# Recurrent layer of a two-layer encoder: the 19 dense-weight loads issued by ScalarE instead of SyncE

## The chip, the core and the metric

The kernel runs on one core of one Trainium2 chip, in one launch. The metric is device time in microseconds (us), the median of the runs shown; lower is better. The core has five engines that work at the same time, each taking its own instructions in the order of its own queue: TensorE (in the profile PE, with its weight loads as PEld), VectorE (DVE), ScalarE (ACT), GpSimd (POOL) and SyncE (SP). SyncE computes nothing here; it begins transfers. GpSimd begins those transfers that add to what they write. An engine that begins a transfer spends a short instruction on it, called the issue here; the data lands later, and whoever reads it waits for the landing.

## The reference, cut to what matters

The input is x (512 tokens of 1024 values). Layer 0 mixes tokens with a recurrence over 12 heads of 64, in parallel with an attention of 4 heads into 256 memory tokens; layer 1 does the same with chunked attention in place of the recurrence. Each layer ends in an output projection and a gated feed-forward block.

```python
h = rms_norm(x, ln1[0])
p = h @ a_w_in[0]                      # r, k, v of the recurrence, and the memory queries
def step(state, inp):                  # for each of the 512 tokens, 12 heads
    r_t, w_t, k_t, v_t, a_t, b_t = inp
    sa = einsum('bhvk,bhk->bhv', state, a_t)
    state = (state * w_t[:, :, None, :] + sa[..., None] * b_t[:, :, None, :]
             + v_t[..., None] * k_t[:, :, None, :])
    return state, einsum('bhvk,bhk->bhv', state, r_t)
mix = group_norm(y) * ... * g
mo  = memory_attention(q_mem, mem_n, w_mem_kv[0])
x = x + concatenate([mix, mo]) @ w_out[0]
x = x + conv_glu(rms_norm(x, ln2[0]), ...)
```

The change touches only layer 0 up to its output projection: the part with `a_w_in`, and the first two column tiles of `w_out[0]`.

## The kernel before, in words

**Dense products.** A weight tile is 128 x 1024 values of float32 (512 KB). It is loaded into a buffer called `wraw` (two buffers, so a load may begin when the reader of the tile before last has finished). `split_w` (lines 204 to 221) then makes two tiles from it: `whi`, a copy rounded to TensorE's float32 format, by ScalarE (line 207), and `wlo`, the rest. There are two ways to the rest. With `lo` off, VectorE subtracts (`wlo` = raw - `whi`, line 215). With `lo` on, ScalarE writes the raw tile, scaled by -1 and rounded (line 212) and GpSimd begins a transfer that adds the same weight tile from memory to it (line 213), so VectorE has no part in it. `whi` and `wlo` have three buffers each. `dense` (line 248) then issues 16 matmuls with `whi` (lines 257 and 258) and 8 with `wlo` (line 261) into one bank of results (`psd`).

**Where a load is begun.** `raw_w` (line 224) allocates the `wraw` buffer and issues the load, always on SyncE (line 226). `load_w` calls it and splits.

**The recurrent layer.** The 12 heads are six pairs. Per pair there are three generators: `prepare` (three projections k, r and v, each with its own weight tile; decay, keys, bonus), `front` and `back` (the chunked form of the recurrence, in many small matmuls). `weave` traces a step of whichever generator is furthest behind its share of the estimated cost. In stage st (0 to 4) it weaves `front` of pair st, `prepare` of pair st+1 and `back` of pair st-1. A last weave holds the two last `back`s, the last `front`, two projections for the memory queries (`q_mem`), the memory attention and two of the eight tiles of the output projection (`out_ahead`). In `prepare`, a projection takes the tile that was loaded ahead and asks for the next one (line 1174 and following) before its own matmuls are traced.

**Who orders the queues.** The traced order is only a preference: the framework draws up the queue of each engine from dependencies, free buffers and priorities. `tc.issue_after`, `tc.keep_in_program_order` and `tc.high_priority` are the kernel's own marks for places where that order is held down.

**The switch `lo_on`.** `lo_on[0]` is 0 at first, set to 1 at line 1596 before stage 0 and back to 0 at line 1635 after the last weave. While it is 1, `load_w` takes the second way to `wlo` (`prepare` passes `lo` itself: for the first two tiles of the second pair it is off).

**The small transfers.** `keys` turns a small triangular system through DRAM: ScalarE copies blocks into `Lc` (line 1235), eight small transfers write them to `d` (line 1238), four read them back re-arranged as `Lr` (line 1244), VectorE runs a recursion of 15 steps on `Lr` and `X` (lines 1246 to 1266, tiles `Xu`, `Xsa`, `Xsb`), four transfers write `X` to `d2` (line 1272) and four read it back as `Tc` (line 1276), which `front` uses. Also `wa` (line 1154), `g2` (line 1470) and the mixer's result (`mixd`, line 1527) go through SyncE's queue, as did the weight loads.

Of the kernel before, what the change touches and what calls it, by code (L numbers as in the profile page):

```python
# [133 lines left out]
def trunk_kernel(ctx, tc, A, out):  # L134
    nc = tc.nc
    PE, V, SC, GP = nc.tensor, nc.vector, nc.scalar, nc.gpsimd
# [5 lines left out]
    def wtile(name, dt=F32R, tag=None, at=None, slot=None):  # L142
        if name in turns:
            n = turns[name] if slot is None else slot
            while (name, n) in held:
                n = (n + 1) % 3
            turns[name] = (n + 1) % 3
            tag = f"{name}{n}"
            at = W_AT[name] if at is None else at
        else:  # L150
            at = at or 0
        t = wp.tile([P, 1056], dt, name=name, tag=tag or name, bufs=1 if name in turns else 2)
        return t[:, at:at + 1024]
# [47 lines left out]
    lo_on = [0]  # L201
    raw_at = [None]
# [20 lines left out]

    def raw_w(src, n=1024):
        raw = wtile("wraw", F32)
        raw_at[0] = nc.sync.dma_start(raw[:, :n], src)
        return raw[:, :n]

    def load_w(src, n=1024, lo=None, at=None):
        return split_w(raw_w(src, n), n, src if (lo_on[0] if lo is None else lo) else None, at=at)  # L230
# [204 lines left out]
    def ffn(l, hp, U, T, new_x, xT, after=None, tokens=None):  # L435
# [199 lines left out]
        def ending():  # L635
            j = NFF - 1
            last7 = made[j - 1]
            src = A["ffn_in"][l, j]
            made[j - 2].end2()
            wg = split_w(raw_w(src[0]), 1024, None, keep, hold=True)  # L640
            yield
            wg[2]()
# [9 lines left out]
            pg = ps_d()  # L652
            run(dense(pg[:], [(wg[:2], KO)], pair_of(Uh, Ul)))
            wv_raw = raw_w(src[1])
            last7.end1()
            last7.endr()
# [922 lines left out]
    with tc.issue_after(norm_at[0].ins):  # L1579
# [5 lines left out]
        for m in range(KD):  # L1585
            src = memT[m // 4][:, m % 4]
# [470 lines left out]
```

## Time and profile before

| | us |
|---|---|
| median of 3 runs (lowest, highest) | 1273.2 (1271.75, 1273.56) |
| the profiled execution | 1271.7 |
| its span (first to last instruction) | 1269.9 |
| VectorE busy in the span | 1031.8 |
| ScalarE busy in the span | 839.7 |
| GpSimd busy in the span | 151.2 |

The profile is of one execution, so sums are made against its 1271.7 us and then moved to the median. A busy time does not count issues of transfers, branches or semaphores. In a list of waits, a line says which engine and line sat idle, which instruction ended that, the total in us, how often, and the longest. In a timeline, a row is: start, duration, engine, line, operation, tiles, count; a bracket at the end holds the idle time before it and what ended it. A row with a count above 1 merges neighbours. "DMA to landing" is the time from the issue until the data is there.

### The profile page before, as it was taken

To read this page: it belongs to the slowest core of one execution; us is meant where nothing else is said; L and a number is where in the kernel's file an instruction comes from. 1 tells how busy PE (TensorE), PEld (TensorE's weight loads), DVE (VectorE), ACT (ScalarE), POOL (GpSimd) and SP (SyncE) were. 2 spreads that over 40 slices of the span, in tenths; PEclk is the share of its full clock that TensorE was granted. 3 is DMA by queue.
4 is the path that set the end of the run, shared out by engine and by line. 5 is a ranking of instruction groups with operands and counts; after the bars stand their busy time and mean duration, and the time that the engine had idled before them with its cause. 6 is when DMAs were issued, how large, how long until landed. Compare 5 with 4: busy or idle time off the path is not lost.

```text
span 1269.9 us, 26429 instructions
## 1 busy us (share of the span) xinstructions
PE 1227.0 (97%) x10420; PEld 1077.7 (85%) x10420; DVE 1031.8 (81%) x1958; ACT 839.7 (66%) x1396; POOL 151.2 (12%) x180
## 2 busy tenths in 40 slices
PE   9999999999998999999999999999999999999997
PEld 7787777777788999999888878777789999998886
DVE  7976677765678999999886976658889999999785
ACT  6567668756466777776664676767767777765662
POOL 1000000000001222220120000000002322211200
PEclk9999999999999999999999999999999999999999
DMA  6355444353064889885994332233428899977971
GB/s 207 102 171 119 96 107 92 83 118 102 6 194 114 195 214 204 201 204 131 304 223 130 108 101 67 84 108 133 133 50 192 212 208 196 201 165 254 245 178 67
DMA packets 95293, 191.10 MB, mean 150 GB/s; under 512 B 22080, under 2 KB 30400, under 8 KB 95168
## 3 DMA queue, kind: packets, MB, share of 16 engines
q1 hardware_dynamic: 68592, 129.14, 31.9%
q0 software_dynamic: 26576, 60.26, 27.0%
q8 instruction: 82, 1.34, 0.4%
q14 instruction: 43, 0.35, 0.1%
HBM read 173.15 MB, written 6.29 MB: 141 GB/s over the span
## 4 chain that ended last, share of the span: by engine, by line
PE 46%; DVE 23%; ACT 11%; issue 10%; DMA 10%; SPq 0%; POOL 0%; ACTq 0%; DVEq 0%; POOLq 0%
PE psf L718 7%; DMA wlv<-in_ffn_in_dram 5%; PE psd L261 4%; PE psf L723 3%; PE psf L452 3%; PE psd L257 3%; PE psd L258 3%; PE psd L718 3%; ACT whi L517 2%; DVE wlo L215 2%; PE psf L454 2%; DVE raw L504 2%; DVE wlo L522 2%; PE psd L723 1%; DVE raw L513 1%
## 5 line engine op out<-in xcount | busy, mean ns | idle before, releaser
L517 ACT CAST whi<-raw 128x1024 fp32r<-128x1024 f32 (+1 forms) x168 | 151.0, 939 | 52.1 <-DVE raw L509 26.4
L452 PE MATMUL psf<-th,whi 128*128 128x256 f32 x672 | 159.6, 276 | 4.2 <-ACT tmp L573 2.1
L452 PE MATMUL psf<-tl,whi 128*128 128x256 f32 x672 | 159.1, 275 | 0.0
L452 PEld LDWEIGHTS psf<-th,whi 128*128 128x128 f32 x672 | 128.8, 192 | 5.3 <-ACT tmp L573 2.8
L207 ACT CAST whi<-wraw 128x1024 fp32r<-128x1024 f32 x84 | 87.3, 1045 | 66.8 <-PE psd L258 33.9
L452 PEld LDWEIGHTS psf<-tl,whi 128*128 128x128 f32 x672 | 129.0, 192 | 0.0
L522 DVE TENSOR_TENSOR wlo<-raw,whi 128x1024 fp32r<-128x1024 f32 (+1 forms) x108 | 109.0, 1011 | 6.5 <-ACT whi L517 6.5
L257 PE MATMUL psd<-r1h,whi 128*128 128x512 f32 x264 | 104.1, 395 | 0.1
L258 PE MATMUL psd<-r1l,whi 128*128 128x512 f32 x264 | 101.6, 386 | 0.0
L215 DVE TENSOR_TENSOR wlo<-wraw,whi 128x1024 fp32r<-128x1024 f32 x67 | 81.6, 1218 | 20.9 <-ACT whi L207 20.5
L708 ACT CAST whi<-raw 128x1024 fp32r<-128x1024 f32 (+1 forms) x52 | 49.3, 951 | 54.2 <-PE psf L718 27.1
L709 DVE TENSOR_TENSOR wlo<-raw,whi 128x1024 fp32r<-128x1024 f32 (+1 forms) x52 | 56.5, 1096 | 30.7 <-ACT whi L708 29.0
L454 PE MATMUL psf<-th,wlo 128*128 128x256 f32 x504 | 77.3, 275 | 0.0
L261 PE MATMUL psd<-r1h,wlo 128*128 128x512 f32 x264 | 70.4, 389 | 1.1 <-DVE wlo L215 1.1
L544 ACT ACTIVATE tmp<-tmp,vec 128x512 f32<-128x512 f32 x44 | 36.0, 818 | 52.3 <-DVE tmp L531 52.2
L489 POOL DMA_DIRECT2D wlv<-in_ffn_in_dram x40 | 60.0, 1500 | 55.4 <-DVE wlo L522 54.3
L454 PEld LDWEIGHTS psf<-th,wlo 128*128 128x128 f32 x504 | 66.6, 192 | 0.0
L452 PE MATMUL psf<-r2l,whi 128*128 128x256 f32 x252 | 59.8, 276 | 1.1 <-DVE r2l L316 1.1
L452 PE MATMUL psf<-r2h,whi 128*128 128x256 f32 x252 | 60.2, 277 | 0.0
L452 PE MATMUL psf<-r1h,whi 128*128 128x256 f32 x252 | 59.8, 276 | 0.0
L452 PE MATMUL psf<-r1l,whi 128*128 128x256 f32 x252 | 59.7, 275 | 0.0
L257 PEld LDWEIGHTS psd<-r1h,whi 128*128 128x128 f32 x264 | 49.8, 189 | 9.6 <-issue 2.5
(610 smaller groups left out, 3562.1 us busy)
## 6 DMA issues: line engine op xcount, KB each, us to landing
raw<-in_ffn_in_dram SPq DMA_DIRECT2D x42, 512.0 KB, 4.2
raw<-in_ffn_in_dram SPq DMA_DIRECT2D x84, 256.0 KB, 4.8
wlv<-in_ffn_in_dram POOLq DMA_DIRECT2D x40, 512.0 KB, 8.5
raw<-in_ffn_out_dram SPq DMA_DIRECT2D x30, 512.0 KB, 5.2
raw<-in_ffn_out_dram POOLq DMA_DIRECT2D x24, 512.0 KB, 9.4
wraw<-in_wA_dram SPq DMA_DIRECT2D x20, 512.0 KB, 4.2
wraw<-in_w_out_dram SPq DMA_DIRECT2D x16, 512.0 KB, 3.9
wraw<-in_ffn_outp_dram SPq DMA_DIRECT2D x16, 512.0 KB, 4.6
```

Of the source, the lines that this page charges most:

```text
L207: high = lambda: pin(SC.copy(hi[:, :n], raw))
L215: pin(V.tensor_tensor(lo[:, :n], raw, hi[:, :n], op=ALU.subtract))
L257: PE.matmul(ps, wh[:, j * P:(j + 1) * P], ah, start=start and n == 0, stop=False)
L258: dense_at[0] = PE.matmul(ps, wh[:, j * P:(j + 1) * P], al, start=False, stop=False)
L261: dense_at[0] = PE.matmul(ps, wl[:, j * P:(j + 1) * P], moving(act(k))[0], start=False, stop=stop and n == len(ks) - 1)
L452: PE.matmul(ps, wh[:, o + k * P:o + k * P + P], x[k][n], start=k == n == 0, stop=False)
L454: PE.matmul(ps, wl[:, ol + k * P:ol + k * P + P], x[k][0], start=False, stop=k == 3)
L489: GP.dma_start(self.low[:].rearrange("p (a s) -> p a s", a=2), self.second, accum_op=ALU.add)
L517: keep(SC.copy(hi[:, :n], self.pair(what) if n > S else self.raw[:, what]))
L522: keep(V.tensor_tensor(lo[:, :n], self.pair(what) if n > S else self.raw[:, what], hi[:, :n], op=ALU.subtract))
L709: V.tensor_tensor(lo, s_, hi, op=ALU.subtract)
L718: PE.matmul(ps[:], a[:, k0 + i, ts], woven(hi[:, i * S:i * S + S]), start=bool(first) and (first is True or t in first) and a is act[0] an ...
```

## The change

While `lo_on[0]` is 1, `raw_w` issues the load on ScalarE (`SC`) instead of SyncE, so the load goes into ScalarE's queue of instructions and from there into ScalarE's queue of transfers. Otherwise it stays with SyncE. Nothing else is edited.

```diff
     def raw_w(src, n=1024):
         raw = wtile("wraw", F32)
-        raw_at[0] = nc.sync.dma_start(raw[:, :n], src)
+        raw_at[0] = (SC if lo_on[0] else nc.sync).dma_start(raw[:, :n], src)
         return raw[:, :n]
```

The loads that are traced while the switch is on are three for each of the pairs two to six (15), two for the memory queries and two for the output projection: 19 of 512 KB each. The other six loads of that output projection, and everything after it, keep SyncE.

## The prediction, made before the changed kernel was run

> **What bounds the kernel now.** I read the page first, then the one stretch that the change touches. From the page: the span, the busy line of TensorE, and the engines' shares of the chain that ended last.
>
> ```profile
> span 1269.9 us, 26429 instructions
> PE 1227.0 (97%) x10420; PEld 1077.7 (85%) x10420; DVE 1031.8 (81%) x1958; ACT 839.7 (66%) x1396; POOL 151.2 (12%) x180
> PE 46%; DVE 23%; ACT 11%; issue 10%; DMA 10%; SPq 0%; POOL 0%; ACTq 0%; DVEq 0%; POOLq 0%
> ```
>
> TensorE is busy nearly all the time, and the queue of SyncE (SPq) and that of ScalarE (ACTq) are nowhere on the chain. So I asked for the engines' work from 75 to 310 us, the stretch in which the moved loads and their readers lie, and then for what TensorE waited for there (engine and line, total us, times, longest).
>
> ```profile
> core 0: us, PE busy (x) PEld busy (x) DVE busy (x) ACT busy (x) POOL busy (x), PEclk, DMA share, GB/s
> 75.00:310.00 235.00, 225.46 (x3513) 177.76 (x3512) 165.38 (x470) 160.53 (x311) 14.75 (x17) 1.00 0.49 111
> ```
>
> ```profile
> PE pss L1395 <- ACT Y L1384: 1.8, 5, 0.5
> ...
> PE pss L1102 <- ACT tmp L1502: 0.7, 1, 0.7
> PE pss L1102 <- ACT tmp L1211: 0.7, 1, 0.7
> ...
> PE pss L1454 <- ACT Tt L1448: 0.7, 1, 0.7
> ...
> PE pss L1126 <- ACT tmp L274: 0.5, 2, 0.3
> PE pss L1289 <- ACT tmp L274: 0.5, 1, 0.5
> PE psl L234 <- ACT g2h L1503: 0.4, 1, 0.4
> ```
>
> In 235.00 us TensorE is idle for 235.00 - 225.46 = 9.5 us. That is all that any change to this stretch can win while the matmuls stay the same. In 12 places, 5.3 us together (the seven rows), ScalarE was the last to arrive; no row names a load of weights. ScalarE itself is busy for 160.53 of the 235 us (68%), in 311 instructions.
>
> Next, the raw weight tiles in the stretch of the moved loads: their issues on SyncE (ns, shortest/median/longest), how long they take to land, and who waited for them.
>
> ```profile
> L226 SPq DMA_DIRECT2D wraw<-in_wA_dram x17: 328/351/1518, 75.6 to 237.6; - x17
> L226 SPq DMA_DIRECT2D wraw<-in_w_out_dram x2: 333/378/422, 253.4 to 265.7; - x2
> ...
>   ACT whi L207: 5.5, 3
> ...
> DMA to landing us min/median/max: 3.4/4.2/6.7
> ```
>
> 17 + 2 = 19 loads, as the diff says. Only three of them were waited for, by the cast on ScalarE, 5.5 us in all.
>
> **The change part by part.** *Removed from SyncE:* 19 issues of 0.351 us, 6.7 us, and the waits in front of them, as SyncE's own list of waits shows.
>
> ```profile
> SPq L226 <- ACT wlo L212: 41.1, 15, 6.7
> ...
> SPq L226 <- DVE wlo L215: 13.1, 1, 13.1
> ```
>
> SyncE stood 54.2 us in front of loads whose buffer was still being read. That in itself is worth nothing, as SyncE computes nothing; what counts is whether a small transfer stood behind it that somebody was waiting for. I looked at all readers of the small tiles `Lr` and `Tc`. `Tc` was waited for once, in the last pair (not behind a moved load), `Lr` once, in the second pair. Here are SyncE's timeline, the chain's piece, VectorE's row and the summary for `Lr`.
>
> ```profile
> 111.91 0.35 SPq L226 DMA_DIRECT2D wraw<-in_wA_dram  x1
> 112.44 1.73 SPq L1244 DMA_DIRECT2D Lr<-d  x4
> ```
>
> ```profile
> 113.73 6.67 DMA Lr<-d
> ```
>
> ```profile
> 120.52 0.36 DVE L1253 TENSOR_TENSOR Xu<-Lr,cst 128x120 f32<-128x120 f32 x1 [2.80 <-DMA Lr<-d]
> ```
>
> ```profile
> DMA to landing us min/median/max: 1.6/1.7/6.7
> ```
>
> A load of 512 KB was begun 0.53 us before the four `Lr` transfers of 32 KB, in the same queue, and the last `Lr` took 6.67 us where the median is 1.7 us; VectorE idled for 2.80 us. The row shows the small transfer held up by the load ahead of it. [...]
>
> How much of the 2.80 us reaches TensorE? TensorE's timeline around it has two idle places of size.
>
> ```profile
> 119.40 1.44 PE L1454 MATMUL pss<-VT,Tt 64*64 64x128 f32 x16 [0.71 <-ACT Tt L1448]
> ```
>
> ```profile
> 134.47 0.45 PE L1126 MATMUL pss<-tmp,blk 128*128 128x512 f32 x1 [0.71 <-DVE MQ L1467]
> ```
>
> The first was ended by ScalarE and stays. The second was ended by VectorE and may go: gain 0.7 us (bounds: 0, and 2.8 if the whole wait were TensorE's). The rest is hidden under dense matmuls, which fill TensorE whatever VectorE does.
>
> *Added to ScalarE:* 19 issues. The trace has no issue on ScalarE, so the nearest rows are SyncE's: 0.351 us at the median, 1.518 us at the longest. From below, an issue might cost nothing, if it runs while the ScalarE instruction ahead of it is still at work. I take 0.35 us: 6.7 us in all. What of that TensorE feels depends on where they stand. The order is the framework's; that it is not the traced one is seen in a pair of casts that are traced one after the other. These are rows of ScalarE's timeline.
>
> ```profile
> 75.81 1.05 ACT L207 CAST whi<-wraw 128x1024 fp32r<-128x1024 f32 x1 [1.98 <-DMA wraw<-in_w_memv_dram]
> ...
> 121.92 1.04 ACT L207 CAST whi<-wraw 128x1024 fp32r<-128x1024 f32 x1
> ...
> 124.46 1.06 ACT L212 ACTIVATE wlo<-wraw 128x1024 fp32r<-128x1024 f32 x1
> ...
> 164.11 0.59 ACT L1439 COPY VT<-pss 128x512 f32<-128x512 f32 x1 [0.85 <-PE pss L1438]
> ```
>
> I count 25 idle gaps of ScalarE from the first of these rows to the last, in 90 us: with 311 instructions in 235 us that is one gap to about 5 instructions. A delay is passed on to the next gap and swallowed there. With 19 issues among 311 instructions (one in 16), one of the 12 tight places has an issue in the five instructions ahead of it with a chance of 5/16 = 0.3; so some four are hit, at 0.35 us each: 1.3 us. Bounds: 0, and 6.7 us if each issue stands ahead of a tight place. An issue at its longest, 1.518 us, would cost 1.2 us more than that wherever it falls.
>
> *The wait in front of a load moves too.* On SyncE it held up small transfers; on ScalarE it would hold up its casts, copies and exponentials, and through them VectorE and TensorE. But the readers that free a buffer are the cast and the scaled copy (lines 207 and 212), which are ScalarE's own and stand ahead of the load in the same queue: 15 of SyncE's 16 waits above cannot block ScalarE for longer than its own last instruction. The exceptions are the first tiles of the second pair, which VectorE reads (line 215). There the third load goes out as soon as VectorE is done, and its cast is waiting for it:
>
> ```profile
> 82.83 2.28 SPq L226 DMA_DIRECT2D wraw<-in_wA_dram  x2
> ```
>
> ```profile
> 83.55 0.68 ACT L1170 ACTIVATE a<-pss,aw0h 128x512 f32<-128x512 f32 x1
> ...
> 87.32 1.04 ACT L207 CAST whi<-wraw 128x1024 fp32r<-128x1024 f32 x1 [3.09 <-DMA wraw<-in_wA_dram]
> ```
>
> If the load has to stand behind the row at 83.55, it begins at 84.23, 1.4 us later than now, and so does the cast. I put that at 0, since dense matmuls of tiles already cast lie over it; without that cover it costs 1.4 us. For the later loads lateness is cheap: the one begun at 130.55 is cast at 144.46, which is 13.9 us against 4.2 us to land.
>
> ```profile
> 130.55 1.52 SPq L226 DMA_DIRECT2D wraw<-in_wA_dram  x1
> ```
>
> ```profile
> 144.46 1.05 ACT L207 CAST whi<-wraw 128x1024 fp32r<-128x1024 f32 x1 [3.14 <-PE psd L258]
> ```
>
> This cast did not wait for its load but for TensorE, to give back a `whi` buffer.
>
> *Sum:* +1.3 - 0.7 + 0 = +0.6 us on 1271.7 us, so 1272.3 us for an execution like the profiled one. The median stands 1273.2 - 1271.7 = 1.5 us above that execution, so the forecast is **1273.8 us**: no change that can be told, as 0.2% (2.5 us) is about what a measurement of this kernel can tell from no change. [...]
>
> **The rivals.** *Slower: issues ahead of ScalarE's tight places.* The 12 places where TensorE already waits for ScalarE are short handovers, and a scaled copy that frees a buffer often has such work right behind it. With every issue felt at 0.35 us the cost is 6.7 us, with the third load's 1.4 us it is 8.1 us: 1281.3 us. It decides from 2.5 / 0.35 = 7 of the 19 issues on. For it: ScalarE has 68% of the stretch filled. Against it: a gap after each five instructions.
>
> *Faster: the small transfers get a free queue.* The pieces of the chain `d`, `Lr`, `X`, `d2`, `Tc` come sooner in every pair, and VectorE and TensorE move up. Price: at most the idle time that ScalarE did not end, 9.5 - 5.3 = 4.2 us: 1269.0 us. For it: the 6.67 us. Against it: in the other pairs nobody waited for `Lr`.
>
> *Slower by far: loads come too late.* If the order puts each load right ahead of its own cast, ScalarE stands for 4.2 + 0.35 us at each, 86 us in all, against the 74.5 us in which it is idle; at least 12 us would be left over: 1285 us or more. Against it: 13.9 us of lead in the row above, and an order that is not the traced one.
>
> *The change does nothing at all* can't be, as 19 loads are traced under the switch; that they land later or earlier without anybody noticing is the forecast.
>
> **How the numbers follow.** The forecast, within 2.5 us: 0.38. Slower through the tight places: 0.31, and through late loads 0.04, together 0.35 slower. Faster through the free queue: 0.27; this includes that the queues are drawn up anew on all engines, which can fall out either way by as much as the 9.5 us of idle time allows. The range reaches from the faster rival's 1269.0 us to the slower rival's 1281.3 us and leaves out late loads and what a redrawn order could win beyond 4.2 us. The likeliest case's own range is 1270.7 to 1275.7 us.
>
> **What would show it.** Right: SyncE's issues of `wraw` in this stretch are gone; the longest `Lr` landing is near 2 us and VectorE's 2.80 us wait is gone; ScalarE has 19 issues of about 0.35 us; TensorE's idle time from 75 to 310 us stays within 2.5 us of 9.5 us. Wrong: TensorE's waits ended by ScalarE grow from 5.3 us to over 8 us (slower rival); TensorE's idle time falls to 7 us or less (faster); the casts at line 207 wait for their loads much longer than 5.5 us (late loads).

## The result, and the profile after

The changed kernel takes 1276.28 us (median of 14 runs, 1272.95 to 1281.28), the kernel before 1270.77 us beside it (14 runs). The ratio is 1.0042 with a 95% interval of 1.0028 to 1.0056: slower by 0.42%, some 5.5 us. The profiled execution of the kernel after took 1275.98 us.

The span and the engines' shares of the chain, from the page of the kernel after, look much like those of before, but for TensorE:

```profile
span 1274.2 us, 26428 instructions
PE 54%; DVE 20%; ACT 9%; issue 8%; DMA 8%; SPq 0%; POOL 0%; ACTq 0%; DVEq 0%; POOLq 0%
```

From 75 to 310 us (columns: length, TensorE's busy time and instructions, granted clock, DMA share, GB/s):

```profile
75.00:310.00 235.00, 224.46 (x3458) 0.99 0.49 111
```

TensorE's idle time there went from 9.5 to 235.00 - 224.46 = 10.5 us, which doesn't explain 5.5 us. The granted clock of 0.99 is the hint: a matmul at half clock counts as busy (further down, the slice from 104 to 105 us: busy for 1.00 of 1.00 us at a clock of 0.50). What TensorE waited for in that stretch:

```profile
PE pss L1102 <- ACT tmp L1211: 4.4, 1, 4.4
PE pss L1395 <- ACT Y L1384: 1.7, 4, 0.5
...
PE psl L234 <- ACT g2h L1503: 0.4, 1, 0.4
```

One wait of 4.4 us is new; before, the same place waited 0.7 us. It hangs on ScalarE, so the next view is ScalarE's timeline there:

```profile
91.65 0.70 ACT L1182 ACTIVATE krv<-tmp,om 128x512 f32<-128x512 f32 x1
96.72 0.36 ACTq L226 DMA_DIRECT2D wraw<-in_wA_dram  x1
97.12 1.07 ACT L1348 COPY VT<-pss 128x512 f32<-128x512 f32 x2 [4.77 <-DMA d2a<-Xsa]
98.08 0.73 ACT L1206 ACTIVATE kn<-krv,kneg 128x512 f32<-128x512 f32 x1
98.85 0.63 ACT L1211 ACTIVATE tmp<-kn 128x512 f32<-128x512 f32 x1
```

The row with the bracket is a copy from PSUM, which has no use for `d2a`. What stood is the instruction ahead of it, the issue of the sixth moved load; everything behind it in ScalarE's queue stood too. The chain says the same, in order of time:

```profile
91.92 4.73 DMA d2a<-Xsa
...
96.72 0.36 ACTq L226
...
97.12 1.07 ACT VT L1348 x2
98.19 0.63 ACT kn L1206
...
98.85 0.64 ACT tmp L1211
...
99.53 1.87 PE pss L1102 x8
```

Why a weight load waits for `d2a`, a small write to DRAM with which it shares no data, is not shown: the trace names the transfer that ended the wait and not the reason. In the kernel before, the sixth load did not wait for it. It was begun on SyncE at 92.39 us, with `d2a` still on its way (the `Tc` reads, which wait for `d2a`, began at 96.70 us), and nothing that computes is queued behind it there. The move redraws the order in which the transfers are begun, and which transfer the issue waits for may hang on that; the experiments try it.

The same matmuls on TensorE, before and after; the bracket is the idle time ahead of them:

```profile
96.06 1.05 PE L1102 MATMUL pss<-cst,tmp 128*128 128x2 f32 x8 [0.72 <-ACT tmp L1211]
```

```profile
99.53 1.87 PE L1102 MATMUL pss<-cst,tmp 128*128 128x2 f32 x8 [4.38 <-ACT tmp L1211]
```

The idle time is about half the price. TensorE's granted clock behind it, kernel after (same columns):

```profile
97.00:98.00 1.00, 0.00 (x0) 1.00 1.10 224
98.00:99.00 1.00, 0.00 (x0) 0.62 0.93 262
99.00:100.00 1.00, 0.47 (x3) 0.50 0.96 366
...
104.00:105.00 1.00, 1.00 (x4) 0.50 0.00 0
105.00:106.00 1.00, 1.00 (x9) 0.96 0.00 0
```

Read as mixtures of the 1.00 and the 0.50 of the slices around them, 0.62 means that the clock fell at 98.24, and 0.96 that it came back at 105.08: 6.84 us. TensorE worked from 99.53 on, so 5.55 us of it at a clock of 0.50. The six matmuls of line 261 behind the wait took 2.91 us there and 1.54 us before; at half speed, by estimate, the 5.55 us lose 2.8 us. With 4.38 - 0.72 = 3.66 us more idle time that makes 6.4 us. Two rows of SyncE show how much arrives, from before and from after; the first `d` transfer of the second pair comes 5.6 us later:

```profile
106.16 4.60 SPq L1238 DMA_DIRECT2D d<-Lc  x8
```

```profile
111.79 4.49 SPq L1238 DMA_DIRECT2D d<-Lc  x7
```

`d2a` was begun 0.5 us earlier here than before (89.26 against 89.73 us), so some 6.1 us were lost in between. The first raw load of the feed-forward block is still 5.8 us later (347.09 before, 352.89 after). So the loss is made at about 100 us and kept up to there. At the end of these two executions 4.3 us of it are left (spans of 1269.9 and 1274.2 us); where the rest went isn't shown.

### The profile page after: what moved, and what is told of

The parts are those of the page before. It is cut to its first block, busy times and chain, and to the rows that moved or that the text cites. A ratio compares the mean times of both kernels' runs of the same rounds, so it can differ in the third digit from the quotient of the medians.

```text
span 1274.2 us, 26428 instructions
## 1 busy us (share of the span) xinstructions
PE 1230.0 (97%) x10420; PEld 1082.3 (85%) x10420; DVE 1031.6 (81%) x1958; ACT 842.0 (66%) x1396; POOL 151.5 (12%) x180
## 4 chain that ended last, share of the span: by engine, by line
PE 54%; DVE 20%; ACT 9%; issue 8%; DMA 8%; SPq 0%; POOL 0%; ACTq 0%; DVEq 0%; POOLq 0%
PE psf L718 7%; PE psf L452 7%; PE psd L261 4%; DMA wlv<-in_ffn_in_dram 4%; PE psd L257 4%; PE psf L723 3%; PE psf L454 3%; PE psd L258 3%; PE psd L718 3%; DVE wlo L215 2%; ACT whi L517 2%; DVE raw L504 2%; PE psd L723 1%; PE pss L1837 1%; DVE wlo L522 1%
```

## The experiments

Theory A: the one wait of the sixth load's issue for another transfer, with the lower clock behind it. Theory B: the loss is spread over the 19 issues on ScalarE and the queues that were redrawn on all engines. Theory C: the sixth load costs at its place on ScalarE, whichever transfers are begun ahead of it. The loads are counted in the order in which they are traced; `loads[0]` in the diffs is that number.

**All but the sixth.**

```diff
-        raw_at[0] = (SC if lo_on[0] else nc.sync).dma_start(raw[:, :n], src)
+        raw_at[0] = (SC if lo_on[0] and loads[0] != 6 else nc.sync).dma_start(raw[:, :n], src)
```

> The sixth moved load is begun by SyncE again, the other 18 by ScalarE. [...] Without that issue on ScalarE nearly the whole loss goes: 4 to 6 us faster than the kernel after, within 2 us of the kernel before (ratio to it 0.999 to 1.0015); the wait of VT for d2a and the clock of 0.50 between 99 and 105 us are gone, and the first d<-Lc of the second pair is at about 106 us. Theory B, the loss is spread over the 19 issues on ScalarE and the changed order of the other queues: 18 of 19 parts stay, ratio to the kernel before 1.003 to 1.0055.

Measured: 1273.18 us, ratio to before 1.0020 (1.0008 to 1.0033). About half of the loss went, not nearly all. The wait for `d2a` is gone, but a new one stands some microseconds further on. ScalarE and TensorE in this run:

```profile
103.50 1.05 ACT L207 CAST whi<-wraw 128x1024 fp32r<-128x1024 f32 x1 [4.71 <-DMA wraw<-in_wA_dram]
```

```profile
107.44 0.68 PE L1395 MATMUL pss<-Y,Tn 16*16 16x16 f32 x64 [2.37 <-ACT Y L1384]
```

On SyncE the sixth load now stands behind the four `Tc` reads, which wait for `d2a`, and begins at 97.73 instead of 92.39 us; its cast waits 4.71 us. So the edit put a late load in the place of the wait for `d2a`, and the run tells the theories apart only halfway. The clock fell here too, to 0.50 for 3.4 us. By its time alone this run decides nothing: it lies between the forecasts (A at most 1.0015, B at least 1.003).

**Only the sixth** (`loads[0] == 6`).

> Only the sixth load is begun by ScalarE, the other 18 by SyncE. [...] Theory C, this load on ScalarE costs in itself (its place ahead of VT in ScalarE's order): the loss of the kernel after, ratio 1.003 to 1.005. Theory B (spread over the issues): 1/19 of it, not to be told from none.

Measured: 1269.82 us, 0.9992 (0.9975 to 1.0009), within the 0.999 to 1.001 of theory A and out of reach for theory C's 1.003 to 1.005. With the 18 others on SyncE, the same load on the same engine ahead of the same copy costs nothing:

```profile
93.62 0.39 ACTq L226 DMA_DIRECT2D wraw<-in_wA_dram  x1
94.11 1.04 ACT L1348 COPY VT<-pss 128x512 f32<-128x512 f32 x2
```

No bracket, no idle time, although by SyncE's rows `d2a` was still on its way: its last issue ended at 91.03 + 1.94 = 92.97 us, and the `Tc` reads, which wait for it, began at 97.74 us. Theory C falls.

**The first six** (`loads[0] <= 6`).

> The first six loads are begun by ScalarE, the later 13 by SyncE. [...] Theory A: nearly the whole loss, 4 to 6 us over the kernel before, ratio 1.003 to 1.0055, with TensorE idle for about 4.4 us at 95 to 99 us and a clock of 0.50 behind it. Theory B: six of 19 parts, 1 to 2 us, ratio 1.0005 to 1.002.

Measured: 1277.58 us (6 runs), 1.0048 (1.0029 to 1.0067), as theory A has it and out of reach for theory B's 1.0005 to 1.0020. The profile is of the shortest of the six executions (1272.71 us; the others took 1277.39 us and more), and even there ScalarE's wait is about as long as in the kernel after:

```profile
94.92 0.36 ACTq L226 DMA_DIRECT2D wraw<-in_wA_dram  x1
95.32 1.07 ACT L1348 COPY VT<-pss 128x512 f32<-128x512 f32 x2 [4.71 <-DMA d2a<-Xsa]
```

**One more transfer** is begun between the writes to `d2a` and the sixth load.

```diff
-        for h in range(2):
-            nc.sync.dma_start(wa[HS[h]], A["wa2"][i].rearrange("p (a f) -> p a f", a=2))
+        for a_, b_ in ((0, 64), (64, 96), (96, 128)) if i == 3 else ((0, 64), (64, 128)):
+            nc.sync.dma_start(wa[a_:b_], A["wa2"][i].rearrange("p (a f) -> p a f", a=2)[a_ % 64:a_ % 64 + b_ - a_])
```

> All 19 loads are begun by ScalarE as in the kernel after; one load of SyncE between the writes to d2a and the sixth load (wa, for i = 3) is cut from two transfers into three of the same bytes. [...] Theory A: ScalarE's wait at the sixth load falls from 4.77 us to 0 to 2 us, TensorE's idle time behind it from 4.4 us to under 2 us, no slice of 2 us has a clock under 0.9 there, and the time is 3 to 6 us below that of the kernel after, ratio to the kernel before 0.999 to 1.0015. [...] Theory B: the number of issues on ScalarE is the same, the time too: ratio to the kernel before 1.003 to 1.0055.

Measured: 1274.69 us, 1.0028 (1.0015 to 1.0041): not down to 1.0015, and by the time alone not to be told from the kernel after (1.0028 to 1.0056) or from theory B. The profile tells more. The sixth load waits for the fifth now, by name, and no longer for `d2a`; the fifth took 7.0 us to land, where it took 5.1 us in the kernel after. ScalarE, TensorE and the clock:

```profile
96.35 1.07 ACT L1348 COPY VT<-pss 128x512 f32<-128x512 f32 x2 [3.63 <-DMA wraw<-in_wA_dram]
```

```profile
98.75 1.05 PE L1102 MATMUL pss<-cst,tmp 128*128 128x2 f32 x8 [3.30 <-ACT tmp L1211]
```

```profile
100.00:101.00 1.00, 1.00 (x5) 0.64 0.16 47
...
103.00:104.00 1.00, 1.00 (x5) 0.65 0.00 0
```

The wait changed its name with one more transfer ahead of it and got 1.1 us shorter (3.63 against 4.77 us), and the clock stayed low from 100.28 to 103.70, 3.4 us instead of 6.8. So one more transfer begun ahead of the issue changed what it waited for, which fits theory A; what would be left of the wait was expected too small (0 to 2 us).

**From the seventh on** (`loads[0] >= 7`), the complement of the first six.

> The first six moved loads are begun by SyncE as in the kernel before, the later 13 by ScalarE as in the kernel after: the complement of the run that moved the first six. Theory A (one wait, at the sixth load): no loss, ratio to the kernel before 0.9985 to 1.001; TensorE idles about as before between 75 and 310 us (9 to 11 us) and its clock stays at 1.00 there, although 13 of the 19 issues stand on ScalarE and the orders of TensorE, VectorE and ScalarE behind them are redrawn. Theory B (spread over the issues and the redrawn order): 13 of 19 parts of the loss, ratio 1.0025 to 1.004.

Measured: 1271.22 us, 1.0010 (0.9999 to 1.0021). TensorE is busy for 227.88 of the 235 us and its clock is 1.00 (columns as in the prediction's row of this stretch):

```profile
75.00:310.00 235.00, 227.88 (x3511) 180.29 (x3511) 164.69 (x469) 160.50 (x311) 14.75 (x17) 1.00 0.48 111
```

13 issues and three engines' redrawn queues are worth 0 to 2.7 us, not theory B's 0.25% and more.

**Filling the gap**, two runs: extra matmuls ahead of those that wait, first in their own PSUM bank, then in one that is free.

```diff
-            for t in range(4):
-                PE.matmul(ps[:, 2 * t:2 * t + 2], sq[:, t * P:(t + 1) * P], C(sel), start=True, stop=True)
+            for t in range(-NFILL * (sel == "hs1" and fill), 4):
+                PE.matmul(ps[:, 2 * t:2 * t + 2], sq[:, t * P:(t + 1) * P], C(sel), start=True, stop=True) if t >= 0 else PE.matmul(ps[:, :P], C("ident"), C("ident"), start=True, stop=True)
```

(`fill` is true for the second pair; `NFILL` is 11. The second run has `NFILL` 18 and the bank `pf`, taken from `psl`.)

> The kernel after, with 11 extra matmuls (128x128, their sums are overwritten) put on TensorE directly ahead of the matmuls of L1102 that wait 4.4 us; nothing else is reordered. They fill most of the idle time and shorten nothing. Theory A1: of the loss of about 5.5 us, some 3 us are the lower granted clock that followed the idle time; with TensorE kept busy the clock stays over 0.9 between 97 and 107 us and the kernel is 2 to 4 us faster than the kernel after, ratio to the kernel before 1.001 to 1.0028, though it does more work and ScalarE waits as long as in the kernel after (4.8 us). Theory A2: the lower clock follows something else (the transfers in flight, the kind of matmul), or costs nothing on the path: the clock falls to 0.50 again, or the time stays at 1.0035 to 1.0055.

Measured: 1280.97 us (6 runs), 1.0085 (1.0061 to 1.0108). The bank was in use: the extra matmuls waited 5.27 us for ScalarE's copy of `VT` out of it and then ran at half clock on the path (0.50 from 99 to 103 us, 0.67 from 103 to 105 us).

```profile
99.70 4.91 PE L1102 MATMUL pss<-cst 128*128 128x128 f32 x22 [5.27 <-ACT VT L1348]
```

> The kernel after with 18 extra matmuls (128x128, their sums are not used) directly ahead of the matmuls of L1102 that wait; other than in the run before, they write a PSUM bank that is free then (psl), so that they wait for nothing and can run while TensorE stands. At full clock 18 of them take about 4.0 us (0.22 us each: 11 took 4.91 us at half clock in the run before). Theory A1 (the idle time brings the lower clock): TensorE's idle time ahead of L1102 falls to under 2 us, the clock stays over 0.9 between 97 and 107 us, and the time is 2 to 4 us below the kernel after: ratio to the kernel before 1.001 to 1.0028. Theory A2 (the lower clock has another cause or costs nothing on the path): the clock falls to 0.50 again though TensorE is busy, or the time stays at 1.0035 to 1.0055.

Measured: 1277.46 us (6 runs), 1.0060 (1.0042 to 1.0079). This time they ran in the gap, but the gap had grown; ScalarE and TensorE:

```profile
99.48 1.07 ACT L1348 COPY VT<-pss 128x512 f32<-128x512 f32 x2 [7.25 <-DMA d2a<-Xsa]
```

```profile
94.57 4.29 PE L1102 MATMUL psl<-cst 128*128 128x128 f32 x36
101.89 1.05 PE L1102 MATMUL pss<-cst,tmp 128*128 128x2 f32 x8 [3.03 <-ACT tmp L1211]
```

ScalarE's wait for `d2a` was 2.2 and 2.5 us longer than in the kernel after in the two filled runs (7.01 and 7.25 us against 4.77), for a reason that stays open; in the second, 3.03 us of TensorE's idle time were left, and the clock fell to 0.55 to 0.59 from 103 to 107 us (slices of 2 us). The expected gain didn't come, and the run is no fair test of A1, as the idle time didn't go. That a busy TensorE would have kept its clock through this wait is not shown.

**All 19 on GpSimd.**

```diff
-        raw_at[0] = (SC if lo_on[0] else nc.sync).dma_start(raw[:, :n], src)
+        raw_at[0] = (nc.gpsimd if lo_on[0] else nc.sync).dma_start(raw[:, :n], src)
```

> All 19 loads are begun by GpSimd, in the queue in which the loads of the low halves (L213) stand already; ScalarE and SyncE begin none of them, and TensorE's order is that of the kernel before. [...] Theory A: no loss, ratio to the kernel before 0.998 to 1.0015; if SyncE's queue freed of the loads is worth anything, up to 0.7 us of gain, which is too little to tell. Rival: in one queue with the low halves' loads, which wait for the casts, a load starts late: casts of L207 wait for their loads over 5 us longer than before (5.5 us there), and the time is 1.003 or more.

Measured: 1274.74 us, 1.0037 (1.0023 to 1.0051), against theory A's 1.0015. So theory A's forecast for this run failed. The rival fell as well: its time came, but the casts waited 4.0 us in all for their loads, not over 10. The profiled execution (span 1268.9 us) shows no loss; a second one follows.

> The run with all 19 loads begun by GpSimd once more, for a second profile: its first profiled execution was no longer than that of the kernel before, its median 0.37% longer. If the loss is a wait that not every execution has, a slower execution shows it in 75 to 310 us as a TensorE wait of 2 us or more with a lower clock behind it; if the loss lies elsewhere, this part of the profile shows 9 to 11 us of idle time as before.

Measured: 1275.19 us, one execution. It shows a third way to the same end. SyncE, TensorE and the clock:

```profile
100.48 2.02 SPq L1276 DMA_DIRECT2D Tc<-d2a  x4
```

```profile
106.11 0.20 PE L1378 MATMUL pss<-Tc,Lc 32*32 32x16 f32 x2 [1.70 <-DMA Tc<-d2a]
106.84 1.37 PE L1378 MATMUL pss<-Tc,Lc 32*32 32x16 f32 x62 [0.52 <-DMA Tc<-d2a]
```

```profile
106.00:107.00 1.00, 0.36 (x4) 0.83 0.19 23
107.00:108.00 1.00, 1.00 (x62) 0.50 0.17 17
```

The `Tc` reads begin at 100.48 instead of 96.70 us, because `d2a` took 8.8 us from its last issue (91.69 us), where it took 4.9 us before. TensorE stands for 1.70 and 0.52 us, and the clock is low from 106.66 to 113.48 us. In the first profile the reads began at 97.87 us, TensorE waited 1.7 us, and the clock stayed at 1.00. GpSimd's loads land in 7.1 and 7.0 us (medians from 84 to 106 us in the two profiles) where SyncE's take 4.0; that they crowd `d2a` is likely, but wasn't tried by itself.

**The sixth on GpSimd, the other 18 on ScalarE.**

```diff
+        raw_at[0] = ((nc.gpsimd if loads[0] == 6 else SC) if lo_on[0] else nc.sync).dma_start(raw[:, :n], src)
```

> 18 of the 19 loads are begun by ScalarE as in the kernel after; the sixth is begun by GpSimd, right behind the load of the low half that stands there already, at about 91 us and so in time. The orders of TensorE, VectorE and SyncE are those of the kernel after, word for word. Theory A: ScalarE no longer waits for d2a, TensorE does not idle there, and nearly the whole loss goes: ratio to the kernel before 0.999 to 1.0015; the rest over 1.000 is the share of the other 18 loads. Theory B (issues on ScalarE and redrawn orders): both are nearly all still there, ratio 1.003 to 1.0055.

Measured: 1271.43 us, 1.0016 (1.0004 to 1.0028), a hair above theory A's 1.0015 and below theory B's 1.003. This is the clean form of the first experiment, since the load isn't late (begun at 91.10 us; its cast at 100.61 us waited for TensorE and not for it). ScalarE goes through without a bracket:

```profile
92.06 1.05 ACT L1348 COPY VT<-pss 128x512 f32<-128x512 f32 x2
93.00 0.64 ACT L1211 ACTIVATE tmp<-kn 128x512 f32<-128x512 f32 x1
```

One load on another engine takes 1.0042 to 1.0016. The other 18 cost 0.16% (0.04 to 0.28%), 0.5 to 3.6 us, by the medians; the profile shows no loss in the stretch of the moved loads (table at the end of this section), and where it arises stays open.

**Only the eighth** (`loads[0] == 8`), for the prediction's gain at `Lr`.

> Only the eighth load is begun by ScalarE, the one that stands directly ahead of the small transfers into Lr in SyncE's queue in the kernel before. The term of the prediction: the longest landing of Lr falls from 6.7 us to near 2 us, VectorE's wait for it of 2.80 us goes, and 0 to 1 us is gained. Its rival, from the trace of the kernel after: a load in another queue takes the same share of the DMA engines from Lr, whose longest landing stays above 5 us where the load still starts ahead of it; the time is within 0.1% of the kernel before either way, so that the landing decides and not the time.

Measured: 1268.85 us, 0.9988 (0.9972 to 1.0004). VectorE doesn't wait for `Lr` any more; the longest landing is 4.4 us. What moved is the start of the load: it is begun behind the `Lr` transfers now, no longer ahead of them. SyncE and ScalarE, and then the landings of `Lr` in the kernel after and in this run:

```profile
111.44 1.70 SPq L1244 DMA_DIRECT2D Lr<-d  x4
113.31 0.39 ACTq L226 DMA_DIRECT2D wraw<-in_wA_dram  x1
```

```profile
DMA to landing us min/median/max: 1.7/2.4/5.6
```

```profile
DMA to landing us min/median/max: 1.6/1.7/4.4
```

In the kernel after the load began at 118.86 us, 0.23 us before the fourth of those issues ended (117.38 + 1.71), and the longest landing was 5.6 us; in the run from the seventh on 0.17 us before, 5.2 us; here 0.17 us behind, 4.4 us. Four more runs have the load behind: 0.07 us and 4.5 us (one more transfer), 0.19 us and 3.7 us (the sixth on GpSimd), 0.21 us and 2.2 us (the sixth and the eighth), 1.57 us and 2.1 us (all but the sixth). So a queue of its own didn't shield `Lr`, and the start just behind it only in part (the median over all pairs is 1.7 us); but VectorE waited 1.04 and 0.58 us in the two runs with the load begun ahead, and not at all in those with the load begun behind.

**The sixth and the eighth** (`loads[0] in (6, 8)`).

> The sixth and the eighth load are begun by ScalarE, the other 17 by SyncE: the two single moves that came out a little under the kernel before, together. [...] If both gains are real and add up, the ratio to the kernel before is 0.997 to 0.999; if they are noise, 0.9985 to 1.001.

Measured: 1268.64 us, 0.9985 (0.9972 to 0.9998): 0.15% below the kernel before, just clear of no change, and far below the kernel after. It lies on the border of the two expectations (up to 0.999 for real gains, from 0.9985 for noise), and it is the lowest of a dozen versions, so that chance may have a part in it. VectorE doesn't wait for `Lr`, and ScalarE has no idle time in front of either issue (90.44 and 110.57 us).

**The stretch alone.** The medians hold what happens in the whole kernel. The profiles also give the time from the first `d` transfer of the first pair, which is begun ahead of all moved loads, to the first raw load of the feed-forward block. One execution each:

| | us | against before |
|---|---|---|
| before | 279.72 | |
| after | 285.29 | +5.6 |
| the first six | 285.41 | +5.7 |
| filling the gap, two runs (more work) | 288.70 and 287.66 | +9.0 and +7.9 |
| one more transfer | 283.88 | +4.2 |
| all but the sixth | 282.64 | +2.9 |
| all 19 on GpSimd, first and second profile | 280.17 and 283.96 | +0.5 and +4.2 |
| from the seventh on | 279.86 | +0.1 |
| the sixth on GpSimd, the other 18 on ScalarE | 279.67 | 0.0 |
| only the sixth | 279.12 | -0.6 |
| only the eighth | 278.71 | -1.0 |
| the sixth and the eighth | 277.98 | -1.7 |

The runs in which ScalarE stands in front of the sixth load lose 4.2 us or more here. With 18 of the 19 loads on ScalarE and the sixth elsewhere and in time, nothing is lost, against theory B.

## Why the prediction was right or wrong

The time, 1276.28 us, lies in the range of 1269.0 to 1281.3 us, but the likeliest case, no change that can be told, did not come. It came out slower, and not by the rival that stood for slower. That the range holds it is luck: its upper end was there for issues ahead of tight places, and no term of the prediction was a wait for another transfer.

- **The step that failed** is "15 of SyncE's 16 waits above cannot block ScalarE for longer than its own last instruction". As a statement on those 16 waits it holds. But it took SyncE's list of waits for the list that ScalarE would get. On ScalarE the issue of the sixth load stood for 4.77 us until `d2a` had landed, whose data it doesn't use; with one more transfer ahead of it, it stood for 3.63 us until the fifth load had. The prediction looked at data and buffers alone; what ties such an issue to another transfer is not shown.
- **The price of a wait** was taken as its length. At 4.4 us of idle time the granted clock fell to 0.50 for 6.84 us, and the matmuls behind paid 2.8 us more, by the estimate above.
- **The issue term** of +1.3 us was sized well: an issue on ScalarE took 334 ns (median of 17; 393 at most) where 351 had been put in, and the 18 other loads cost 0.5 to 3.6 us by the medians, with all that was redrawn, and nothing in the profiled stretch.
- **The `Lr` term** of -0.7 us has the right sign at most: the run with the eighth load alone gained -0.04 to 0.28%, in which 0.7 us (0.06%) can't be told from nothing. The sign that was named (a longest landing near 2 us) did not come in the kernel after: 5.6 us, with 1.04 us of VectorE's wait left. That a queue of its own lets `Lr` pass the load did not show: with the eighth load begun ahead on ScalarE the longest landing was 5.6 us here and 5.2 us in the run from the seventh on.
- **The third load** at 0: its cast waited 2.31 us, and TensorE was busy for 20.00 of the 20 us from 75 to 95 us. Right.
- **The rivals.** Late loads: the casts waited 2.8 us in all for moved loads, less than the 5.5 us before; refuted for this change. Slower through tight places: its sign came (waits of TensorE ended by ScalarE went from 5.3 to 8.7 us), but 4.4 us of that is the one wait behind the sixth load, and 13 issues without it measured 0.10% (-0.01 to 0.21%).
- **The sign for being right**, idle time within 2.5 us of 9.5 us, came too (10.5 us) while the kernel lost 5.5 us. It was a bad sign: a stretch with fixed ends holds less work when everything shifts, and half-clock matmuls count as busy.

## What to carry to other kernels

When transfers are moved to an engine that computes, look in the trace at what each issue waits for there, and not only at data and buffers: here one issue of 19 stood for 4.77 us until a transfer had landed whose data it doesn't use, and that engine's work stood behind it. A bracket that names a transfer the waiting instruction doesn't use points to the issue ahead of it. Moving only two loads with no idle time in front of their issues, one of them begun behind a small transfer and not ahead of it, cost nothing where the whole move cost 0.42%; the gain over the kernel before, 0.15%, is too near to nothing to build on. Compare milestones (when a given transfer or matmul starts), not idle time in a fixed stretch.

## What the runs showed of the hardware that was not expected

In five profiles a single idle gap of TensorE, or two close together, was followed by a granted clock of 0.50, and for stretches of two lengths: 6.8 us in the kernel after (4.38 us idle), with the first six (4.6 us idle) and in the second GpSimd profile (1.70 and 0.52 us idle, 0.2 us of work between), 3.4 us with one more transfer (3.30 us idle) and with all but the sixth on ScalarE (2.37 us idle). What decides between the two lengths stays open. After a wait of 1.7 us in the first GpSimd profile, and after the 0.72 us in the kernel before, it stayed at 1.00. In the slices of these runs the clock was 0.50 or 1.00, or between the two at an edge, and the shortest idle time with a fall behind it was 1.70 + 0.52 = 2.2 us. Once it fell when the work had already begun again: with one more transfer TensorE worked from 98.75 us on, and the clock fell at 100.28.
